# A second-level product for q's and k's first cells, decay products spaced further from their banks, and part of W_b's sums moved beside z

## The chip, the cores and the metric

The kernel runs on one core of one Trainium2 chip. Its time is the device time in microseconds of one execution; the times given are medians of several. All engines of the core run side by side: TensorE (PE in the profile, its weight loads PEld), VectorE (DVE), ScalarE (ACT), GpSimd (POOL), and SyncE (SP), which here does nothing but issue transfers.

## The reference

One layer of a decoder trunk for 1024 tokens and a model width of 1024. A combined projection of the normalised input gives all branches; branch A is a gated linear attention with decays, branch B a short gated convolution.

```python
h = rms_norm(x, norm_mix_g[i])
proj = jnp.einsum('bsd,dc->bsc', h, w_in[i])
(q, k, v, z_a, gk_low, cb, cc, xc, z_c, g_a, g_c) = jnp.split(proj, idx, axis=-1)
gk = log_sigmoid(gk_low @ w_gk2[i] + b_gk[i]) / GATE_NORMALIZER
o = gla_chunked(q, k, v, gk)                 # 4 heads, chunks of 64 tokens
y_a = (rms_norm(o, gla_norm_g[i]) * silu(z_a)) @ w_branch_a[i]
u = causal_dwconv(cc * xc, conv_w[i])
y_c = (cb * u * silu(z_c)) @ w_branch_c[i]
merged = sigmoid(g_a + b_ga) * y_a + sigmoid(g_c + b_gc) * y_c
x = x + merged @ w_out[i]
x = x + sigmoid(rms_norm(x, norm_ple_g[i]) @ w_ple_gate[i]) * (p[i] @ w_ple_proj[i])
return rms_norm(x, norm_final_g)
```

## The kernel before, in words

**Products.** Every large projection is done in quadrants by the Strassen-Winograd scheme: seven products of quadrant sums stand for eight. One product of one `Cell` is 12 matmuls 512 columns wide: four steps of 128 in the contraction, each of three matmuls (high by high, low by high, high by low part of operands that are split into two fp32r parts). A cell keeps three banks of PSUM: X, V and Y. Product 0 goes to X, product 1 to V, product 2 to Y (a copy of X), and DVE and ACT take the quadrants out of the banks as they are finished (`cons`). The weight sums of a product ("operand", with the names `T`, `raw`, `hi`, `lo`) are made by DVE and ACT up to seven products ahead, in a ring of eight.

**Second level.** `Deep` does one product of a pair of cells by seven smaller products, each of six matmuls of 256 columns: 42 of 256 in place of 24 of 512. It runs in two stages, one of 24 matmuls and one of 18, and between the two DVE adds four times and ACT copies twice on the banks (`dw` is the scratch tile, so `cc00dw` is the one of the pair cc0, xc0 for product 0). It needs "turned" quarters of h, which `quarters` loads.

**Phases.** In order of time: the norm and the small products until about 74 us; v (until 159 us) and z_a (tiles `za`, until 236.4 us), both by `wide`, which does four cells at once and stores z's silu; then q0 and k0 one after the other, q1 and k1 as a pair, the convolution's cells cc, xc, zc, cb in pairs until 596 us; the merge gates with the attention between them; then the branches' output products, the output projection and the gate of the per-layer embedding.

**The decays.** `decays(half)` makes `lowp`, 16 matmuls with the low-rank gate weights, and then four `zp`, one matmul each, whose banks DVE empties at once (`c<-zp`). They have a tag "o" with two banks, one of which the wide product beside them holds. `zp` and `lowp` are put between the matmuls of v and z.

**W_b.** The gate's weights (`wb`) are read in 16 pieces of 512 KB into the tile `wt`; each piece gets four subtractions of 128x256 and its sums are stored to `wtd` in DRAM, four stores of 128 KB (w = 0) or more (w = 1). In the kernel before, all 16 are woven in beside the convolution's cells.

**The order.** Nothing is issued as it is written: all operations are recorded (so that nearly all carry the line L508), `set_dues` gives each a due time counted back from the end, less its `hurry`, and `put_in_order` runs a small plan with costs per operation and puts each engine's instructions in the order of that plan. The order of the main matmuls is that in which they are recorded; the side ones (`lowp`, `zp`, attention) go in when the plan thinks they are ready, `apart` microseconds behind the release of their bank. `weave(generator, n)` records a generator's steps between products, so that `yield 7` waits seven of those steps. SP issues transfers in one queue.

Of the kernel before, what the change touches and what calls it, by code (L numbers as in the profile page):

```python
# [16 lines left out]
P = 128  # L17
# [502 lines left out]
def kernel(  # L520
# [216 lines left out]
    class Cell:  # L737
# [3 lines left out]
        def __init__(self, name, side, src, res, cons, prods=ORDER, begin=None, s1=None, u2=None, s5=None, fresh=(), mixed=False):  # L741
            self.name, self.side, self.src, self.res, self.cons = name, side, src, res, cons
            self.prods, self.begin, self.after = list(prods), begin, None
            self.get = {"u2": u2, "s5": s5}
            self.s1, self.seed, self.ready, self.halves = s1, None, lambda k: True, None
            self.raw, self.ring, self.order, self.Y, self.deep = [None] * 4, {}, None, None, {}
# [35 lines left out]
        def by_halves(self, k):  # L782
# [4 lines left out]
            for n, acc in enumerate((self.Y, self.Z)):  # L787
# [8 lines left out]
                else:  # L796
                    self.halves(0, n, acc[:, cs])

        def run(self, k):
            if k == self.prods[0]:  # L800
                if self.begin:
                    self.begin()
            if k == 0:
                self.X = bank(self, 0)
                self.product(0, self.X, True)
                self.Y = bank(self, 1)
                nc.scalar.copy(self.Y, self.X)
            elif k == 1:
                if self.seed is not None:
                    self.Y = bank(self, 1)  # L810
                    nc.scalar.copy(self.Y, self.seed)
                self.V = bank(self, 2)
                self.product(1, self.V, True)
                self.c22 = self.taken("s5", self.V)
            elif k == 2:
                self.product(2, self.Y, False)
                self.c12 = self.taken("u2", self.Y)
                if self.halves:
                    self.Z = psm.tile([P, 512], F32, tag=f"m{3 * (1 - self.set)}", name=f"{self.name}Z")
                    nc.scalar.copy(self.Z[:, 256:], self.Y[:, 256:])  # L820
            elif k == 3:
                self.product(3, self.X, False)
                self.cons(0, 0, self.X)
            elif k == 5:
                self.product(5, self.V, False)
                tt(self.c12, self.V, self.c12, op=ALU.add)
                self.cons(0, 1, self.c12)
# [12 lines left out]
    class Deep:  # L840
# [53 lines left out]
        def run(self, k):  # L894
# [16 lines left out]
            else:  # L911
# [3 lines left out]
                for c, t in ((a, self.a), (b, self.b)):  # L915
                    if self.k:
                        c.V = t
                        c.c22 = c.taken("s5", t)
                    else:
                        c.X = t  # L920
                    if self.k or 1 not in c.deep:
                        c.Y = bank(c, 1)
                        nc.scalar.copy(c.Y, c.X)

    def line_up(groups):
# [3 lines left out]
        todo = []  # L929
        for g in groups:  # L930
            own = [(g[s], k) for s, k in (g[0].order or [(s, k) for k in g[0].prods for s in range(len(g))])]
            if g[0].deep and 1 not in g[0].deep:
                todo.insert(len(todo) - 1, (g[0].deep[0], 0))
                own.insert(1, (g[0].deep[0], 1))
            elif g[0].deep:
                at = len(todo)
                g[0].deep[1].behind = [(c, j) for c, j in todo[-2:] if j == 6]
                for m, (k, n, left) in enumerate(((0, 0, 5), (0, 1, 3), (1, 0, 2), (1, 1, 0))):
                    todo.insert(at - left + m, (g[0].deep[k], n))
            todo += own  # L940
# [31 lines left out]
    def ev(name):  # L972
        return ep.tile([P, 512], F32, tag="ev", name=name, bufs=3)
# [222 lines left out]
    def wide(name, w, cons, first, second, more_s, more_u):  # L1196
# [89 lines left out]
        for b in range(4):  # L1286
            cons(1, 0, b, Y[b])

    with phase("v", [ph["prep0"]]) as qp:
        def v_cons(i, j, b, src):  # L1290
            hi = qp.tile([P, 512], F32R, tag="vhi", name=f"vhi{i}_{j}_{b}", bufs=2)
# [4 lines left out]

        def z_cons(i, j, b, src):
            t = ev(f"sz{i}_{j}_{b}")
            act(t, src, AF.Silu)
            store(szd[j][i][:, b], t.rearrange("p (h d) -> p h d", h=2))  # L1300

        smask = qp.tile([P, HALF], F32, name="smask")
# [5 lines left out]
        tt(gdif, graw[:, 4:8, :], graw[:, 0:4, :], op=ALU.subtract)  # L1308


        glw = qp.tile([P, 12, 4, 32], F32R, name="glw")
        for i in range(4):
            split(glw[:, 0:8, i, 0:16], glw[:, 0:8, i, 16:32], graw)
            split(glw[:, 8:12, i, 0:16], glw[:, 8:12, i, 16:32], gdif)
# [5 lines left out]
        def decays(half):  # L1320

            ops = ((0, 0), (4, 3)) if half == 0 else ((0, 1), (8, 6))
            lowp = pso.tile([P, 512], F32, tag="o", name=f"lowp{half}", bufs=2)
            n = 0
            for g0, k in ops:
                for kt in range(4):
                    gl = glw[:, g0 + kt, :, :].rearrange("p a b -> p (a b)")
                    for s in range(2):
                        mm(lowp, gl, hres[k][s][:, kt, :], start=n == 0, stop=n == 15)
                        n += 1  # L1330
            low = qp.tile([P, 512], F32R, tag="low", name=f"low{half}")
# [4 lines left out]
            for hp in range(2):  # L1336
                t1 = [qp.tile([P, HALF], F32, tag="t1", name=f"t1_{half}{hp}{i}", bufs=3) for i in range(2)]
                c = [qp.tile([P, HALF], F32, tag="c4", name=f"c4_{half}{hp}{i}", bufs=4) for i in range(2)]
                for i in range(2):
                    h = 2 * hp + i  # L1340
                    zp = pso.tile([P, 512], F32, tag="o", name=f"zp{half}_{h}", bufs=2)
                    cs = slice(h * P, (h + 1) * P)
                    nc.apart = 0.6
                    mm(zp, g2[:, cs], low, start=True, stop=True)
                    nc.apart, nc.hurry = 0.0, 6.0
                    nc.vector.tensor_scalar(c[i], zp, bgk[:, h:h + 1], None, op0=ALU.add)
# [53 lines left out]
        def extra():  # L1400
# [6 lines left out]
             [(ep, "ev", 3)] * 2, [(ep, "ev", 3), (qp, "wu", 1)])  # L1407
        finish_woven()
        weave(decays(1), 1)
        wide("za", [wv[1, n] for n in range(4)], z_cons, ("m3", "m4", "o", "m5"), ("m0", "m1", "o", "m2"),  # L1410
             [(qp, "vhi", 2)] * 2, [(qp, "vlo", 2)] * 2)
        finish_woven()
        qks = []
# [111 lines left out]
        convs = pairs(convs)  # L1525

    with vp:
        def weights(vp):


            def soon(do, *a, **kw):
                nc.hurry = 60.0
                do(*a, **kw)
                nc.hurry = 0.0

            for w in range(2):
                for kt in range(4):
                    for cs in (slice(0, 256), slice(256, 512)):
                        t = vp.tile([P, 4, 256], F32, tag="wt", name=f"wt{w}_{kt}_{cs.start}")
                        soon(load, t, wb[w][:, :, kt, cs].rearrange("n p c -> p n c"))  # L1540
                        yield 7
                        b11, b12, b22, b21 = (t[:, n] for n in range(4))
                        if w:
                            for n, q in enumerate((b11, b12, b22, b21)):
                                k = kt + 4 * (n >= 2)
                                soon(act, q, q, AF.Copy, scale=gple[:, k:k + 1])
                                if n != 1:
                                    soon(store, wtd[w][4 + (n + 1) // 2][:, kt, cs], q)
                        soon(tt, b11, b12, b11, op=ALU.subtract)
                        yield 1  # L1550
                        soon(tt, b12, b22, b12, op=ALU.subtract)
                        yield 1
                        soon(tt, b22, b22, b11, op=ALU.subtract)
                        yield 1
                        soon(tt, b21, b21, b22, op=ALU.subtract)
                        for n, q in enumerate((b11, b22, b12, b21)):
                            soon(store, wtd[w][n][:, kt, cs], q)
                        yield 2

        gas, gcs = ([Cell(f"{m}{c}", "B", W[f"{m}{c}"], hres, gate_cons(c, bias, dst), prods=(1, 2, 4, 5, 6),  # L1560
                          s1=s1d[n + c]) for c in range(4)]
                    for n, m, bias, dst in ((0, "ga", bga, gad), (4, "gc", bgc, gcd)))
        def quarters(k):
# [10 lines left out]
                back.append((th[:, n], tl[:, n]) if n < 3 or k else (at(hi, 0, 1), at(lo, 0, 1)))  # L1574
            yield 1
            for n in range(4):
                while n == 3 and not k and qks[1].Y is None:
                    yield 1
# [482 lines left out]
```

## Time and profile before

| | |
|---|---|
| median of 3 runs | 1074.16 us (1073.63 to 1074.26) |
| the profiled execution | 1074.43 us |
| its span | 1072.6 us |
| granted clock of TensorE | 0.998 of full speed |
| PE busy | 1063.1 us (99%) |
| DVE busy | 921.5 us (86%) |
| ACT busy | 650.1 us (61%) |
| POOL busy | 45.8 us (4%) |
| moved by DMA | 256.81 MB, 239 GB/s on average |

The profile has a timeline of each instruction (start, duration, engine, line, operation, output and inputs by tile name without buffer numbers, shape, and in brackets the idle time before it and who ended it), the chain of work that ended last, and windows with the busy time of each engine in a stretch (PE, PEld, DVE, ACT, POOL, then the clock, the share of the DMA engines that was busy and GB/s). An "x12" stands for twelve like rows. Matmuls overlap: a 512-wide one is drawn 0.39 us long although the next starts 0.227 us behind it, so distances from start to start count.

### The profile page before, as it was taken

To read this page: it belongs to the slowest core of one execution; us is meant where nothing else is said; L and a number is where in the kernel's file an instruction comes from. 1 tells how busy PE (TensorE), PEld (TensorE's weight loads), DVE (VectorE), ACT (ScalarE), POOL (GpSimd) and SP (SyncE) were. 2 spreads that over 40 slices of the span, in tenths; PEclk is the share of its full clock that TensorE was granted. 3 is DMA by queue.
4 is the path that set the end of the run, shared out by engine and by line. 5 is a ranking of instruction groups with operands and counts; after the bars stand their busy time and mean duration, and the time that the engine had idled before them with its cause. 6 is when DMAs were issued, how large, how long until landed. Compare 5 with 4: busy or idle time off the path is not lost.

```text
span 1072.6 us, 15816 instructions
## 1 busy us (share of the span) xinstructions
PE 1063.1 (99%) x5169; PEld 899.2 (84%) x5169; DVE 921.5 (86%) x1557; ACT 650.1 (61%) x1216; POOL 45.8 (4%) x83
## 2 busy tenths in 40 slices
PE   9999999999999999999999999999999999999996
PEld 7888888888888888888888888888888888888886
DVE  6998987658999998979889788886999888889896
ACT  6778648746654544565556477675766635466555
POOL 0000000000000000000000011120000000012021
PEclk9999999999999999999999999999999999999999
DMA  9963774468767545654557969889586779799963
GB/s 320 357 234 111 237 276 168 155 214 253 224 201 237 188 150 163 209 176 153 196 182 253 291 213 365 296 295 353 190 307 216 286 221 315 243 326 334 308 226 134
DMA packets 164866, 256.81 MB, mean 239 GB/s; under 512 B 13872, under 2 KB 79152, under 8 KB 161840
## 3 DMA queue, kind: packets, MB, share of 16 engines
q1 hardware_dynamic: 164640, 255.55, 70.6%
q8 instruction: 40, 0.66, 0.2%
q14 instruction: 42, 0.34, 0.1%
q10 hardware_dynamic: 144, 0.26, 0.1%
HBM read 166.63 MB, written 89.13 MB: 238 GB/s over the span
## 4 chain that ended last, share of the span: by engine, by line
PE 99%; DVE 0%; ACT 0%; issue 0%; POOL 0%; ACTq 0%; DVEq 0%
PE zaY L508 3%; PE vY L508 3%; PE pe L508 2%; PE vX L508 2%; PE zaX L508 2%; PE zaV L508 2%; PE vV L508 2%; PE op L508 2%; PE kv L508 1%; PE ga1Y L508 1%; PE ga0Y L508 1%; PE ga2Y L508 1%; PE cc2Y L508 1%; PE cc1Y L508 1%; PE cc3Y L508 1%; PE zc2Y L508 1%
## 5 line engine op out<-in xcount | busy, mean ns | idle before, releaser
L508 ACT ACT_TABLE_LOAD x21 | 26.9, 1283 | 1.1 <-PEq L2050 0.7
L508 DVE TENSOR_TENSOR wt<-wt 128x256 f32<-128x256 f32 x64 | 26.9, 421 | 0.2
L508 DVE SCALAR_TENSOR_TENSOR u<-t,vec,u 128x512 f32<-128x512 f32 x32 | 23.9, 750 | 1.8 <-ACT u L508 1.7
L508 ACT ACTIVATE junk<-x 128x512 bf16<-128x512 f32 (+1 forms) x30 | 18.0, 600 | 12.2 <-DVE x L508 11.8
L508 POOL MEMSET t<- 128x2 f32 x8 | 0.8, 99 | 443.9 <-DVE qdl L508 248.2
L508 POOL TENSOR_SCALAR rg<-ms 128x1 f32<-128x1 f32 x8 | 6.4, 796 | 258.8 <-ACT junk L508 258.7
L508 ACT ACTIVATE u<-t,vec 128x512 f32<-128x512 f32 x16 | 11.6, 727 | 6.8 <-DVE t L508 3.9
L508 ACT ACTIVATE og<-op,or 128x256 f32<-128x256 f32 x32 | 13.3, 469 | 2.2 <-POOL or L508 2.2
L508 ACT ACTIVATE junk<-op 128x256 bf16<-128x256 f32 x32 | 12.1, 380 | 3.0 <-PE op L508 2.9
L508 ACT ACTIVATE wt<-wt,vec 128x256 f32<-128x256 f32 x32 | 13.6, 498 | 0.0
L508 ACT CAST S<-S 128x512 fp32r<-128x512 f32 x14 | 8.7, 618 | 7.8 <-PE op L508 6.5
L508 ACT ACTIVATE oq<-oq,vec 128x512 f32<-128x512 f32 x20 | 13.2, 714 | 0.0
L508 PE MATMUL pe<-wpehi,pThi 128*128 128x512 f32 x32 | 13.0, 407 | 0.0
L508 POOL TENSOR_TENSOR or<-or,mhalf 128x2 f32<-128x2 f32 x16 | 12.8, 800 | 1.3
L508 DVE TENSOR_TENSOR szl<-og,szl 128x512 f32<-128x512 f32 x16 | 11.0, 688 | 2.2 <-ACT og L508 2.2
L508 PE MATMUL pe<-wpehi,pTlo 128*128 128x512 f32 x32 | 12.8, 401 | 0.0
L508 PE MATMUL pe<-wpelo,pThi 128*128 128x512 f32 x32 | 12.8, 401 | 0.0
L508 PE MATMUL op<-v,aTh 128*128 128x256 f32 x64 | 12.8, 283 | 0.0
L508 DVE SCALAR_TENSOR_TENSOR S<-S,dds,kv 128x256 f32<-128x256 f32 x24 | 10.4, 477 | 2.7 <-PE kv L508 2.3
L508 DVE TENSOR_TENSOR s<-y,s 128x512 f32<-128x512 f32 x16 | 11.0, 688 | 0.9 <-ACT s L508 0.7
L508 DVE SCALAR_TENSOR_TENSOR hq<-hq,vec,rt 128x512 f32<-128x512 f32 x16 | 11.2, 746 | 0.6 <-PE rt L508 0.6
L508 DVE STREAM_TRANSPOSE oT<-szl 128x512 f32<-128x512 f32 x16 | 11.3, 707 | 0.1
(3568 smaller groups left out, 4322.6 us busy)
## 6 DMA issues: line engine op xcount, KB each, us to landing
wtd<-wt SPq DMA_DIRECT2D x88, 128.0 KB, 2.8
wt<-in_wb_dram SPq DMA_DIRECT2D x16, 512.0 KB, 3.8
v<-vd SPq DMA_DIRECT2D x16, 512.0 KB, 6.0
wgq<-wtd SPq DMA_DIRECT2D x7, 1024.0 KB, 6.7
qk<-qkd SPq DMA_DIRECT2D x12, 512.0 KB, 6.4
vraw<-in_wv_dram SPq DMA_DIRECT2D x20, 256.0 KB, 3.7
zaraw<-in_wv_dram SPq DMA_DIRECT2D x20, 256.0 KB, 4.2
uq<-ud SPq DMA_DIRECT2D x5, 1024.0 KB, 6.2
```

What stands on the lines that cost most here:

```text
L508: o.call(*[place(a) for a in o.args], **{k: place(a) for k, a in o.kw.items()})
```

## The change

It has four parts.

1. q0 and k0 become a pair like q1 and k1, with a second-level product for product 0. The order of products is 1, 5, 2, 3, 4, 6, so both cells' V products run before the bank X is needed; the first stage stands behind the third product, the second behind the next two. Since product 5 comes early, the (0,1) quadrant is put together later, by the new `join`, from X, Y and V. The turned quarters no longer wait for k0's product 0. On PE, 24 matmuls of 512 columns become 42 of 256.
2. The decay's low-rank weights are kept once, and ACT copies them fourfold for each half (`glx`, in the buffer tag "wt"). The plan keeps `lowp`'s first matmul and each `zp` 1.0 us from the release of their bank, where it kept 0 and 0.6.
3. The first five pieces of W_b go beside z, through one buffer, the other eleven stay beside the convolution's cells; their `hurry` falls from 60 to 20.
4. z's first four banks get their tags in another order, and the silu of its first quadrant a `hurry` of 40.

```diff
+        def join(self):
+            self.c12 = self.taken("u2", self.X)
+            tt(self.c12, self.Y, self.c12, op=ALU.add)
+            nc.scalar.copy(self.Y, self.c12)
+            tt(self.c12, self.V, self.c12, op=ALU.add)
+            self.cons(0, 1, self.c12)
...
+            elif k == 2 and self.prods[1] == 5:
+                self.Y = bank(self, 1)
+                self.product(2, self.Y, True)
+                if self.X is not None:
+                    self.join()
...
-                    elif self.k or 1 not in c.deep:
+                    if c.prods[1] == 5:
+                        if c.Y is not None:
+                            c.join()
+                    elif self.k or 1 not in c.deep:
...
-            if g[0].deep and 1 not in g[0].deep:
+            if g[0].deep and g[0].prods[1] == 5:
+                own.insert(3, (g[0].deep[0], 0))
+                own.insert(6, (g[0].deep[0], 1))
+            elif g[0].deep and 1 not in g[0].deep:
...
+    pieces = [(w, kt, slice(c, c + 256)) for w in range(2) for kt in range(4) for c in (0, 256)]
...
+            nc.hurry = 20.0
...
+            nc.hurry = 0.0 if i or j else 40.0
             act(t, src, AF.Silu)
+            nc.hurry = 0.0
...
-        glw = qp.tile([P, 12, 4, 32], F32R, name="glw")
+        glw = qp.tile([P, 12, 32], F32R, name="glw")
...
+            glx = qp.tile([P, 8, 4, 32], F32R, tag="wt", name=f"glx{half}")
+            for n, (g0, _) in enumerate(ops):
+                nc.scalar.copy(glx[:, 4 * n:4 * n + 4], f(glw[:, g0:g0 + 4, None, :].to_broadcast([P, 4, 4, 32])))
...
+                        nc.apart = 0.0 if n else 1.0
                         mm(lowp, gl, hres[k][s][:, kt, :], start=n == 0, stop=n == 15)
...
-                    nc.apart = 0.6
+                    nc.apart = 1.0
                     mm(zp, g2[:, cs], low, start=True, stop=True)
...
+        weave(weights(qp, pieces[:5], 3), 2)
-        wide("za", [wv[1, n] for n in range(4)], z_cons, ("m3", "m4", "o", "m5"), ("m0", "m1", "o", "m2"),
+        wide("za", [wv[1, n] for n in range(4)], z_cons, ("m5", "m4", "o", "m3"), ("m0", "m1", "o", "m2"),
...
-                while n == 3 and not k and qks[1].Y is None:
-                    yield 1
...
-            for g in convs[1:] if k else pairs(qks[2:]) + convs:
+            for g in convs[1:] if k else pairs(qks) + convs:
                 Deep(g, k, turned[k], tq)
+        for c in qks[:2]:
+            c.prods = [1, 5, 2, 3, 4, 6]
...
-            weave(weights(vp), 10)
+            weave(weights(vp, pieces[5:], 7), 10)
...
-        run_groups(single(qks[:2]) + [qks[2:]] + convs, pairs(gas[:2]))
+        run_groups([qks[:2], qks[2:]] + convs, pairs(gas[:2]))
```

On VectorE, this stood between the two second-level stages of the convolution's first pair (`cc00dw` and `xc0X` belong to that stage, `Q` and `kk` to the consumers of q1 and k1; the number behind a name tells buffers of one name apart):

```order
L508 TENSOR_TENSOR cc0lo<-cc0T_3201,cc0hi 128x512
L508 TENSOR_TENSOR Q_1_3180<-q1s_2952,Q_1_3180 128x4x64
L508 TENSOR_TENSOR Q_1_3180<-q1s_2952,Q_1_3180 128x8x64
L508 TENSOR_TENSOR cc00dw<-cc0X,cc00dw 128x256
L508 TENSOR_TENSOR Q_1_3180<-Q_1_3180,dcs 128x4x64
L508 TENSOR_TENSOR xc0X<-xc0X,cc00dw 128x256
L508 TENSOR_TENSOR kk_1_3209<-k1s_3024,kk_1_3209 128x4x64
L508 TENSOR_TENSOR cc00dw<-cc0X,cc00dw 128x256
L508 TENSOR_TENSOR xc0lo<-xc0T_3275,xc0hi 128x512
L508 TENSOR_TENSOR xc0X<-xc0X,cc00dw 128x256
```

And this stands there now:

```order
L508 TENSOR_TENSOR cc0T_3373<-cc0raw_3095,cc0T_3273 128x512
L508 TENSOR_TENSOR xc0lo<-xc0T_3330,xc0hi 128x512
L508 TENSOR_TENSOR Q_1_3376<-q1Y,Q_1_3376 128x8x64
L508 TENSOR_TENSOR cc00dw<-cc0X,cc00dw 128x256
L508 STREAM_TRANSPOSE turned_0_3397<-kk_0_3185 128x4x4x32
L508 TENSOR_TENSOR xc0X<-xc0X,cc00dw 128x256
L508 TENSOR_TENSOR kk_1_3404<-ck_1_3313 128x4x2x64
L508 TENSOR_TENSOR cc00dw<-cc0X,cc00dw 128x256
L508 TENSOR_TENSOR Q_1_3376<-q1Y,Q_1_3376 128x4x64
L508 TENSOR_TENSOR xc0X<-xc0X,cc00dw 128x256
```

The four instructions of the stage (two `cc00dw`, two `xc0X`) are the same; what stands among them is a transpose of k1 and other parts of q1 and k1, and from the first `kk<-k0X` of k0 to the last row there are now 108 instructions, where there were 96.

On TensorE, this stood at the first `lowp` of the second half, in v's product 4:

```order
L508 MATMUL vV_1197<-v5hi_1316,h5lo 128x512
L508 MATMUL vY_1185<-v4hi_1320,h4hi 128x512
L508 MATMUL vY_1185<-v4lo_1332,h4hi 128x512
L508 MATMUL vY_1185<-v4hi_1320,h4lo 128x512
L508 MATMUL vY_1200<-v4hi_1320,h4hi 128x512
L508 MATMUL lowp_1530<-h1hi,glw 128x512
```

And now:

```order
L508 MATMUL vY_1193<-v4hi_1323,h4hi 128x512
L508 MATMUL vY_1193<-v4lo_1330,h4hi 128x512
L508 MATMUL vY_1193<-v4hi_1323,h4lo 128x512
L508 MATMUL vY_1199<-v4hi_1323,h4hi 128x512
L508 MATMUL vY_1199<-v4lo_1330,h4hi 128x512
L508 MATMUL vY_1199<-v4hi_1323,h4lo 128x512
L508 MATMUL vY_1255<-v4hi_1323,h4hi 128x512
L508 MATMUL lowp_1531<-h1hi,glx_1034 128x512
```

`lowp` stands behind seven matmuls of product 4, where it stood behind four.

On SyncE, this stood in z's first part (`zaraw` are the raw z weights, `vd` is where v is stored; buffers by number):

```order
L508 DMA zaraw_3_1769<-in_wv_dram 128x512
L508 DMA vd_1_1786<-vhi_0_0_1778 128x2x256
L508 DMA zaraw_0_1793<-in_wv_dram 128x512
L508 DMA vd_1_1786<-vhi_0_1_1788 128x2x256
L508 DMA vd_1_1786<-vlo_0_0_1797 128x2x256
L508 DMA zaraw_1_1814<-in_wv_dram 128x512
```

And now:

```order
L508 DMA zaraw_3_1776<-in_wv_dram 128x512
L508 DMA wt_0_256_1792<-in_wb_dram 128x4x256
L508 DMA vd_1_1801<-vhi_0_0_1786 128x2x256
L508 DMA vd_1_1801<-vhi_0_1_1798 128x2x256
L508 DMA zaraw_0_1818<-in_wv_dram 128x512
L508 DMA vd_1_1801<-vlo_0_0_1815 128x2x256
L508 DMA zaraw_1_1832<-in_wv_dram 128x512
```

The load of W_b's second piece stands ahead of the next raw z weights; the first piece's four stores stand further up.

More of the change, by code (lines that the diff above doesn't have):

```diff
@@ L745, in __init__ @@
             self.s1, self.seed, self.ready, self.halves = s1, None, lambda k: True, None
-            self.raw, self.ring, self.order, self.Y, self.deep = [None] * 4, {}, None, None, {}
+            self.raw, self.ring, self.order, self.deep = [None] * 4, {}, None, {}
+            self.X = self.Y = self.c12 = None
             (self.steps, self.operand), self.fresh = ring_steps(name, side, self.raw, fresh, mixed), fresh
@@ L825, in run @@
                 self.product(5, self.V, False)
-                tt(self.c12, self.V, self.c12, op=ALU.add)
-                self.cons(0, 1, self.c12)
+                if self.c12 is not None:
+                    tt(self.c12, self.V, self.c12, op=ALU.add)
+                    self.cons(0, 1, self.c12)
             elif k in (4, 6) and self.halves:
@@ L920, in run @@
                         c.X = t
-                    if self.k or 1 not in c.deep:
+                    if c.prods[1] == 5:
+                        if c.Y is not None:
+                            c.join()
+                    elif self.k or 1 not in c.deep:
                         c.Y = bank(c, 1)
@@ L1287, in wide, with weights, soon @@
             cons(1, 0, b, Y[b])
+    pieces = [(w, kt, slice(c, c + 256)) for w in range(2) for kt in range(4) for c in (0, 256)]
+    def weights(pool, some, pace):
+        def soon(do, *a, **kw):
+            nc.hurry = 20.0
+            do(*a, **kw)
+            nc.hurry = 0.0
+        for w, kt, cs in some:
+            t = pool.tile([P, 4, 256], F32, tag="wt", name=f"wt{w}_{kt}_{cs.start}")
+            soon(load, t, wb[w][:, :, kt, cs].rearrange("n p c -> p n c"))
+            yield pace
+            b11, b12, b22, b21 = (t[:, n] for n in range(4))
+            if w:
+                for n, q in enumerate((b11, b12, b22, b21)):
+                    k = kt + 4 * (n >= 2)
+                    soon(act, q, q, AF.Copy, scale=gple[:, k:k + 1])
+                    if n != 1:
+                        soon(store, wtd[w][4 + (n + 1) // 2][:, kt, cs], q)
+            soon(tt, b11, b12, b11, op=ALU.subtract)
+            yield 1
+            soon(tt, b12, b22, b12, op=ALU.subtract)
+            yield 1
+            soon(tt, b22, b22, b11, op=ALU.subtract)
+            yield 1
+            soon(tt, b21, b21, b22, op=ALU.subtract)
+            for n, q in enumerate((b11, b22, b12, b21)):
+                soon(store, wtd[w][n][:, kt, cs], q)
+            yield 2
     with phase("v", [ph["prep0"]]) as qp:
@@ L1298, in z_cons @@
             t = ev(f"sz{i}_{j}_{b}")
+            nc.hurry = 0.0 if i or j else 40.0
             act(t, src, AF.Silu)
+            nc.hurry = 0.0
             store(szd[j][i][:, b], t.rearrange("p (h d) -> p h d", h=2))
@@ L1308 @@
         tt(gdif, graw[:, 4:8, :], graw[:, 0:4, :], op=ALU.subtract)
-        glw = qp.tile([P, 12, 4, 32], F32R, name="glw")
-        for i in range(4):
-            split(glw[:, 0:8, i, 0:16], glw[:, 0:8, i, 16:32], graw)
-            split(glw[:, 8:12, i, 0:16], glw[:, 8:12, i, 16:32], gdif)
+        glw = qp.tile([P, 12, 32], F32R, name="glw")
+        split(glw[:, 0:8, 0:16], glw[:, 0:8, 16:32], graw)
+        split(glw[:, 8:12, 0:16], glw[:, 8:12, 16:32], gdif)
         g2raw = qp.tile([P, 512], F32, tag="low", name="g2raw")
@@ L1326, in decays @@
                 for kt in range(4):
-                    gl = glw[:, g0 + kt, :, :].rearrange("p a b -> p (a b)")
+                    gl = glx[:, n // 2].rearrange("p a b -> p (a b)")
                     for s in range(2):
+                        nc.apart = 0.0 if n else 1.0
                         mm(lowp, gl, hres[k][s][:, kt, :], start=n == 0, stop=n == 15)
@@ L1527 @@
     with vp:
[L1528 to L1549, printed above, removed]
-                        yield 1
[L1551 to L1558, printed above, removed]
         gas, gcs = ([Cell(f"{m}{c}", "B", W[f"{m}{c}"], hres, gate_cons(c, bias, dst), prods=(1, 2, 4, 5, 6),
@@ L1576, in quarters @@
             for n in range(4):
-                while n == 3 and not k and qks[1].Y is None:
-                    yield 1
                 for t, src in zip(back[n], tqd[k][n]):
```

## The prediction

> **What bounds the kernel now.** I read four views of the profile in this order: the busy times and the chain that ended last, TensorE's waits, the chain in order of time at the places that the change touches, and there the timelines of PE (TensorE) and DVE (VectorE).
>
> ```profile
> PE 1063.1 (99%) x5169; PEld 899.2 (84%) x5169; DVE 921.5 (86%) x1557; ACT 650.1 (61%) x1216; POOL 45.8 (4%) x83
> PE 99%; DVE 0%; ACT 0%; issue 0%; POOL 0%; ACTq 0%; DVEq 0%
> PE warm L508 <- DVE zero L508: 1.4, 1, 1.4
> ```
>
> PE is busy for 1063.1 of 1072.6 us and carries 99% of the chain; its one listed wait is 1.4 us at the very start. So the time can fall in two ways only: matmuls take less, or the small holes between them close. It rises by every microsecond that PE is made to wait. The profiled execution took 1074.43 us, its span 1072.6; 1.83 us lie outside the span and I leave them. It stands 0.27 above the median of 1074.16, so I add up against 1074.43 and take off 0.27 at the end.
>
> A full product's quadrant is 12 matmuls 512 columns wide. A second-level product replaces 24 of those by 42 matmuls of 256, in a stage of 24 and a stage of 18. Before has one for k1 and q1, shown here by the chain in order of time (start, duration, what):
>
> ```profile
> 236.38 2.72 PE q0X L508 x12
> 271.73 1.44 PE k1X L508 x12
> 273.17 1.44 PE q1X L508 x12
> 274.61 2.75 PE k0Y L508 x12
> 280.07 0.71 PE k1X L508 x6
> 280.79 1.44 PE q1X L508 x12
> 282.23 2.75 PE k1V L508 x12
> ```
>
> **The change: the pair.** 24 matmuls of 512 cost 2 x 2.72 = 5.44 us. The 42 of 256 cost 274.61 - 271.73 = 2.88 and 282.23 - 280.07 = 2.16; the 12 behind each stage take 2.75 instead of 2.72, 0.06 together. That is 5.10, a saving of **0.34 us** (0.43 if 42 matmuls went at the 18-matmul stage's 2.15 us without those 0.06). A rule speaks against it: the Trainium skill, page "TensorE: Matmul & The Clock Gate", section "Back-to-back issue gap", gives sustained spacings of about 81 ns for 128 columns and 131 for 512; half-width matmuls would then cost nearly as much as full ones, and, put on a line between the two, my estimate is 98 ns for 256 and a loss of 1.0 us. By the same section's isolated gap, N/2.4 + 2.5, it would be a gain of 0.59. The rows above lie between, at 227 ns and 120; they are of this very form, and decide.
>
> **The holes at the decay products.** PE's timeline (start, duration) and the DVE row that frees the bank:
>
> ```profile
> 132.89 1.28 DVE L508 TENSOR_TENSOR vu<-vV,vu 128x512 f32<-128x512 f32 x2
> 133.61 0.39 PE L508 MATMUL vY<-v4hi,h4lo 128*128 128x512 f32 x1
> 133.84 0.39 PE L508 MATMUL vY<-v4hi,h4hi 128*128 128x512 f32 x1
> 134.22 0.50 PE L508 MATMUL lowp<-h1hi,glw 128*128 128x512 f32 x1
> 134.56 0.40 PE L508 MATMUL lowp<-h1lo,glw 128*128 128x512 f32 x1
> 175.81 0.39 PE L508 MATMUL zaX<-za3hi,h3lo 128*128 128x512 f32 x1
> 176.04 0.47 PE L508 MATMUL zp<-low,g 128*128 128x512 f32 x1
> 176.35 0.39 PE L508 MATMUL zaX<-za3hi,h3hi 128*128 128x512 f32 x1
> L508 ACT CAST S<-S 128x512 fp32r<-128x512 f32 x14 | 8.7, 618 | 7.8 <-PE op L508 6.5
> ```
>
> Starts should stand 0.227 apart. `lowp1` starts 0.38 behind its predecessor, the matmul after it 0.34 behind: 0.27 us lost. DVE ends at 134.17, PE starts at 134.22, so that eviction held it, with a hand-off of 0.05. The new order puts `lowp1` three matmuls further back, 0.68 us, more than the 0.27 needed: **-0.27**. The last `zp` loses 0.31 - 0.227 = 0.08; two more matmuls now stand before it, so that hole goes too if the DVE chain before it has not slipped: **-0.08**. The extra broadcast copies of the decay weights are two of ACT per half, and ACT is 61% busy. Three fewer table loads free ACT alone. I cost both at nothing; if the copies' cover failed, `lowp` would wait at most for both, 2 x 0.62 us by the nearest ACT copy of 512 columns in the last row.
>
> **DVE behind the pair.** This is the first price. The new stage stands in a stretch where DVE has no spare time (window: length, PE, PEld, DVE, ACT):
>
> ```profile
> 266.30:317.63 51.33, 51.33 (x258) 43.80 (x258) 51.24 (x100) 28.14 (x58) 0.00 (x0) 1.00 0.69 215
> 266.33 1.02 DVE L508 TENSOR_TENSOR kk<-k0X,kk 128x256 f32<-128x256 f32 x2 [0.27 <-PE k0X L508]
> 267.27 0.41 DVE L508 TENSOR_TENSOR kk<-kk,dcs 128x256 f32<-128x256 f32 x1
> 267.60 0.69 DVE L508 TENSOR_TENSOR q1lo<-q1T,q1hi 128x512 fp32r<-128x512 f32 x1
> 268.20 1.09 DVE L508 STREAM_TRANSPOSE turned<-kk 128x512 f32<-128x512 f32 x1
> 315.87 0.44 DVE L508 TENSOR_TENSOR xc0X<-xc0X,cc00dw 128x256 f32<-128x256 f32 x1
> 317.63 0.28 PE L508 MATMUL xc0X<-h0hi,cc0xc00Bhi 128*128 128x256 f32 x1
> 318.66 0.17 DVE L508 TENSOR_TENSOR dds<-dcs 128x4 f32<-128x4 f32 x1
> 318.74 1.13 DVE L508 STREAM_TRANSPOSE turned<-kk 128x512 f32<-128x512 f32 x1
> ```
>
> At 266.33 DVE has just caught up with PE (it had waited 0.27 for `k0X`). From there it works without a pause until the second `xc0X<-xc0X,cc00dw` ends at 316.31, and PE's second stage for cc0 and xc0 needs that result at 317.63: a margin of 1.32 us. In the new order 108 DVE instructions stand from that `kk<-k0X` up to that `xc0X`, where 96 stood: five more of 512 columns, four more of 256, three more of 4. Start to start these take 0.60 (267.60 to 268.20), 0.33 (267.27 to 267.60) and 0.08 (318.66 to 318.74): 3.00 + 1.32 + 0.24 = 4.56. PE has one more product of 12 between the same two points, 2.72. The margin becomes 1.32 + 2.72 - 4.56 = -0.52, and with the hand-off of 0.05 PE waits **+0.57**. At full durations (0.69, 0.41, 0.17) the added work is 5.60 and the wait 1.6; if DVE comes to the first of these instructions earlier against PE than now (0.27 of waiting) and planned gaps fall well, it is near 0.2. I take 0.57. ACT has 23 us free in that window, which hides the added copy of the join. The turned quarters of h, which the new stage reads, no longer wait for k0's first product, so SP asks for them before any pair needs them.
>
> **Pieces of W_b beside z.** Each piece is a 512 KB load, four subtractions and four stores:
>
> ```profile
> L508 DVE TENSOR_TENSOR wt<-wt 128x256 f32<-128x256 f32 x64 | 26.9, 421 | 0.2
> wtd<-wt SPq DMA_DIRECT2D x88, 128.0 KB, 2.8
> 148.00:152.00 4.00, 4.00 (x19) 3.32 (x18) 4.00 (x8) 2.45 (x6) 0.00 (x0) 1.00 0.57 197
> 150.00:160.00 10.00, 10.00 (x45) 8.27 (x45) 6.41 (x11) 4.34 (x8) 0.00 (x0) 1.00 0.95 320
> 160.00:170.00 10.00, 10.00 (x45) 8.26 (x44) 8.24 (x14) 5.16 (x10) 0.00 (x0) 1.00 0.96 311
> 170.00:180.00 10.00, 10.00 (x45) 7.92 (x43) 10.00 (x18) 9.80 (x15) 0.00 (x0) 1.00 0.15 53
> 169.08 0.69 DVE L508 TENSOR_TENSOR zaT<-zaraw,zaT 128x512 f32<-128x512 f32 x1 [0.48 <-DMA zaraw<-in_wv_dram]
> 169.69 0.68 DVE L508 TENSOR_TENSOR vlo<-vY,vhi 128x512 fp32r<-128x512 f32 x1
> 170.29 0.74 DVE L508 TENSOR_SCALAR c<-zp,vec 128x512 f32<-128x512 f32 x1
> 171.20 0.40 PE L508 MATMUL zp<-low,g 128*128 128x512 f32 x1
> 155.75 0.65 SPq L508 DMA_DIRECT2D zaraw<-in_wv_dram  x1
> 163.79 0.36 SPq L508 DMA_DIRECT2D vd<-vlo  x1
> ```
>
> The 5 x 4 x 0.42 = 8.4 us of DVE leave a later place where PE does not wait, and gain nothing there. In z, DVE has room (82% busy), but the DMA engines do not: 0.95 and 0.96 busy until 170 us, then 0.15. The first piece's four stores and the second piece's load, 1.05 MB, now go into that full stretch ahead of the raw z weights that DVE already waits for at 169.08. At 311 to 320 GB/s they make these 3.3 us later, and about 2 if part of the stores fill the holes before 152 us (0.57 busy there). Weights as such have many microseconds of room; the second `zp` has not: its bank is freed by `c<-zp`, which DVE takes two instructions behind that `zaT`. Before, it ended at 171.03 and `zp` began at 171.20. After, `zaT` starts at 171.1 to 172.4 and `c` ends 1.95 later, 173.0 to 174.3. The new order has this `zp` ten matmuls later, less the 0.27 won: 171.20 + 2.27 - 0.27 = 173.20. PE waits between 0 and 1.1 us; I take the middle, **+0.5**. The two `zp` behind have 13 matmuls, 2.95 us, for five DVE instructions of some 0.6 (3.0 to 3.1), so they keep about the same lag. Below nothing this term can't go: nobody was held by W_b later.
>
> **Sum.** 1074.43 - 0.34 - 0.27 - 0.08 + 0.57 + 0.5 = 1074.81; less 0.27 is **1074.5 us**.
>
> **Rivals.** *All is hidden*: both waits fall away because DVE's order leaves it a microsecond more than my sums; then 1074.43 - 0.69 - 0.27 = **1073.5**. For it speaks that PE's rows show margins of this size met everywhere; against it, that DVE has no free time in the 51 us window.
>
> *SyncE's queue stands in z, and it is slower*: one buffer takes all pieces, so the second piece's load must wait until the first piece's stores have landed, and on SP's in-order queue the raw z weights stand behind it. If SP stood there for one store's 2.8 us on top of the 3.3, `zaT` would come 6.1 later, at 175.2, `c` would end at 177.1, and `zp` would wait 3.9 instead of 0.5: 1074.5 + 3.4 = **1077.9**. For it: that stretch is full and its transfers slow. Against: seven other DMAs are issued between the last store and that load, and SP takes 0.36 to 0.65 us for each, by the last two rows. It is over 0.2% slower once `zaT` comes more than about 4.4 us late.
>
> *The decay products keep their holes* because their banks come free as much later as they now stand: 1074.5 + 0.35 = **1074.9**.
>
> **How the numbers follow.** Chances: my forecast 0.55, all hidden 0.23, holes stay 0.07, SyncE stands 0.13; 0.02 for something unseen that gains more, as holes and pair together hold under 2 us. About 0.2%, 2.1 us, is what a measurement can tell from no change. So faster 0.02, same 0.85, slower 0.13. The low end, 1073.0, is the hidden case with 0.43 for the pair and most of the 0.5 by which the lowest run (1073.63) lies under the median; the high end, 1076.4, is the forecast with both waits at their upper bounds (1.6 and 1.1, so 1076.2) and the beginning of the slower rival.
>
> **What would show it.** Right: after `lowp1`, starts 0.227 apart; two more second-level stages of 2.88 and 2.16 us beside q0 and k0; a hole of about half a microsecond before the second stage of cc0 and xc0, with the `xc0X<-xc0X,cc00dw` of DVE ending 0.05 before it; a hole of up to 1.1 at the second `zp` of z, with the raw z weights landing 2 to 3 us later than now. Wrong: holes in other places (before q1Y or zc0's second stage), a hole of several microseconds in z, or none at all.

## The result: 1076.87 us, 0.26% slower

The changed kernel takes 1076.87 us (median of 10 runs, 1076.01 to 1077.61) beside 1074.05 of the kernel before on the same chip: a ratio of 1.0026, interval 1.0017 to 1.0036. The forecast was 1074.5 with a range up to 1076.4. The profiled execution took 1077.05 us, its span 1075.1.

The page of the changed kernel, busy times and chain:

```profile
PE 1063.4 (99%) x5187; PEld 899.3 (84%) x5187; DVE 926.0 (86%) x1563; ACT 649.7 (60%) x1215; POOL 45.7 (4%) x83
PE 67%; DVE 4%; issue 1%; ACT 0%; DMA 0%; POOL 0%; DVEq 0%; ACTq 0%
```

And TensorE's waits in it (in total, times, longest):

```profile
PE cb0X L508 <- DVE t L508: 1.7, 1, 1.7
PE X L508 <- DVE s L508: 0.4, 1, 0.4
PE xc0X L508 <- DVE xc0X L508: 0.2, 1, 0.2
```

Before, PE carried 99% of the chain and waited for nobody after the start. Now these three waits stand in the list besides that of the start, and the chain leaves PE. The largest is none that the prediction had priced: `cb0X`, the first second-level stage of zc0 and cb0, waits for a DVE product named `t`.

The timelines of DVE and PE there in the kernel before:

```profile
333.67 0.69 DVE L508 TENSOR_TENSOR t<-xc0X,t 128x512 f32<-128x512 f32 x1 [0.89 <-PE xc0X L508]
335.90 0.39 PE L508 MATMUL cc0V<-h5hi,cc0lo 128*128 128x512 f32 x1
336.13 0.28 PE L508 MATMUL cb0X<-turned0h,zc0cb00Shi 128*128 128x256 f32 x1
```

The timelines of PE, GpSimd, ACT and DVE in the changed kernel:

```profile
335.90 0.39 PE L508 MATMUL cc0V<-h5hi,cc0lo 128*128 128x512 f32 x1
337.99 0.36 PE L508 MATMUL cb0X<-turned0h,zc0cb00Shi 128*128 128x256 f32 x1 [1.70 <-DVE t L508]
338.18 0.28 PE L508 MATMUL cb0X<-turned0l,zc0cb00Shi 128*128 128x256 f32 x1
324.45 0.10 POOL L508 MEMSET t<- 128x2 f32 x1 [253.27 <-DMA qkd<-Q]
333.31 0.62 ACT L508 CAST cc0hi<-cc0T 128x512 fp32r<-128x512 f32 x1 [1.40 <-DVE cc0T L508]
334.43 0.58 ACT L508 COPY t<-cc0X 128x512 f32<-128x512 f32 x1
337.15 0.69 DVE L508 TENSOR_TENSOR t<-xc0X,t 128x512 f32<-128x512 f32 x1
```

`cb0X` takes over the bank that held xc0's X. DVE must first multiply that X into `t`, and ACT must before that copy cc0's X there. In the changed kernel DVE does so at 337.15 and ends at 337.84; PE starts 0.15 later, 1.86 late, and loses 0.08 more on the next matmul: 1.94 us. In the kernel before the same product ran at 333.67, as soon as PE had finished xc0's X (DVE stood idle 0.89 us for it), and ended 1.77 us ahead of PE.

The other holes (a hole is the time between two matmul starts beyond the usual 0.227 us, or 0.12 for 256 columns): 0.44 us at the second stage of cc0 and xc0, 0.18 at cc0's Y behind it, 0.23 at v's product 6 (from 147.30 us), and at the attention's first X (from 597.65 us) 0.67 more than the kernel before takes over the same matmuls. The two decay holes of before are closed. Two windows of the kernel before (columns as in the prediction) and the same of the changed one show where DVE's time went:

```profile
236.00:256.00 20.00, 20.00 (x90) 16.57 (x89) 12.79 (x27) 11.37 (x23) 0.00 (x0) 1.00 0.75 240
266.00:337.00 71.00, 71.00 (x358) 60.60 (x357) 68.80 (x133) 38.91 (x79) 0.20 (x2) 1.00 0.69 218
```

```profile
236.00:256.00 20.00, 20.00 (x110) 17.38 (x109) 11.50 (x23) 13.68 (x27) 0.00 (x0) 1.00 0.67 220
266.00:337.00 71.00, 70.11 (x347) 58.81 (x345) 71.00 (x142) 41.15 (x85) 0.20 (x2) 1.00 0.73 227
```

In the first 20 us of q0 and k0 DVE does less than before, 11.50 in place of 12.79; from 266 to 337 us it is busy to the last tenth, 71.00 of 71, where it had 2.2 us to spare. Single, q0 hands DVE its first quadrant at 249.67 us, before k0's first matmul at 255.25, and k0 follows at 266.33; as a pair, both cells' first quadrants come close together, from 260.28 and 262.96 us.

### The profile page after: what moved, and what is told of

It reads as the page before. It is cut to its first block, busy times and chain, and to the rows that moved or that the text cites. A ratio compares the mean times of both kernels' runs of the same rounds, so it can differ in the third digit from the quotient of the medians.

```text
span 1075.1 us, 15853 instructions
## 1 busy us (share of the span) xinstructions
PE 1063.4 (99%) x5187; PEld 899.3 (84%) x5187; DVE 926.0 (86%) x1563; ACT 649.7 (60%) x1215; POOL 45.7 (4%) x83
## 4 chain that ended last, share of the span: by engine, by line
PE 67%; DVE 4%; issue 1%; ACT 0%; DMA 0%; POOL 0%; DVEq 0%; ACTq 0%
PE op L508 2%; PE kv L508 1%; PE ga1Y L508 1%; PE ga0Y L508 1%; PE ga2Y L508 1%; PE cc3Y L508 1%; PE cc2Y L508 1%; PE zc0Y L508 1%; PE zc2Y L508 1%; PE zc1Y L508 1%; PE cc1Y L508 1%; PE gc0Y L508 1%; PE ga3Y L508 1%; PE zc3Y L508 1%; PE xc3Y L508 1%; PE cb2Y L508 1%
```

## The experiments

Each ratio is to the kernel before on the same chip, whose medians were 1073.60 to 1073.95 us. The theories. **A**: the pair puts q0's consumers behind k0's and DVE falls behind until 338 us. **B**: the pieces of W_b, moved and less hurried, upset the order. **C**: the plan thinks k's transposes shorter than they are (0.60 us for 1.02), so that its order is late in fact. **F**: `t` is placed behind q's and k's last work because it lies in memory that they used. **G**, against C and F: DVE has too much to do there in any order. The expectations name two more where they test them: **D**, that `t` stands behind the splits of later operands, or behind ACT, and **E**, that z's banks and the early silu let the pair start.

**The pair undone.** q0 and k0 are single again, all else as changed.

```diff
-        run_groups([qks[:2], qks[2:]] + convs, pairs(gas[:2]))
+        run_groups(single(qks[:2]) + [qks[2:]] + convs, pairs(gas[:2]))
...
-        for c in qks[:2]:
-            c.prods = [1, 5, 2, 3, 4, 6]
```

> The changed kernel with q0 and k0 single again; decays, W_b pieces and z's banks as changed. Theory A (the pair puts q0's consumers behind k0's, DVE falls behind from 260 to 338 us, and PE waits at xc0X, cc0Y and above all at the first second-level stage of zc0 and cb0): the holes there, 2.56 us in the changed kernel, are gone, none above 0.1 between 300 and 345 us; the two decay holes stay closed (-0.35), the new hole of 0.23 at v's product 6 and the 0.4 more at the attention's first X stay; about 1074.3. Theory B (the pieces of W_b in z and their lower hurry upset the order): the holes stay, about 1076.5 or more.

1074.34 us (ratio 1.0006, 0.9997 to 1.0014). No hole above 0.1 from 300 to 345 us, as A says; the hole at v's product 6 stays (0.22), the one at the attention's X is gone too, against the expectation. B falls as a cause of the holes from 300 to 345 us: the pieces are in z here as they are in the changed kernel, and PE waits for nobody after the start:

```profile
PE warm L508 <- DVE zero L508: 1.4, 1, 1.4
```

**The pair alone**, in the kernel before.

> The kernel before with the pair alone. Theory A: a hole of 1.5 to 2.5 us at the first second-level stage of zc0 and cb0, and one of some tenths at xc0X; 1074.05 - 0.34 + 1.5 to 2.6 = 1075.2 to 1076.3. Theory B: no such hole, 1073.7.

1084.21 us (1.0097, 1.0083 to 1.0111), worse than either theory had it. TensorE's waits:

```profile
PE zaY L508 <- ACT zaY L508: 3.5, 1, 3.5
PE k0V L508 <- ACT sz L508: 2.0, 1, 2.0
PE cb0X L508 <- DVE t L508: 0.7, 1, 0.7
PE cc0Y L508 <- ACT cc0Y L508: 0.3, 1, 0.3
```

The holes of A are there, smaller (0.95 and 0.57). But two greater ones stand before them: z's product 2 (the matmuls read `za2`; a later expectation calls it product 4) waits for ACT, and k0's V for ACT's silu `sz`, which still holds the bank that the second cell of the pair wants at once. z's new bank order and the silu's hurry, which I had passed over as costing nothing, looked like the remedy for that, so a later run adds them.

**No pieces in z.** All 16 are beside the convolutions, hurry 20.

```diff
-        weave(weights(qp, pieces[:5], 3), 2)
-            weave(weights(vp, pieces[5:], 7), 10)
+            weave(weights(vp, pieces, 7), 10)
```

> The changed kernel with all 16 pieces of W_b beside the convolutions (hurry 20 as changed). Theory A: the hole at the first stage of zc0 and cb0 stays within half a microsecond of 1.94 us; 1076.0 to 1076.9. Theory B: the holes go, about 1074. The hole at the attention's first X (0.67) tells whether it comes of the pieces: if so it is back at 0.25 or less.

1089.41 us (1.0147, 1.0131 to 1.0162). The hole at cb0X is the same 1.95 us, that at xc0X 0.45: theory A again. The hole at the attention's X is gone. The rest of the loss I had not foreseen; it stands far behind, at the products of the branch's output. The greatest wait there, and that at cb0X:

```profile
PE yc0X L508 <- ACT u0hi L508: 3.1, 1, 3.1
PE cb0X L508 <- DVE t L508: 1.7, 1, 1.7
```

PE comes there before the operand u0 is split. Five more waits of 0.6 to 1.4 us follow up to 791 us, for u0 to u3, and behind the first ones 13 matmuls run at about half the clock (last section): some 12 us together. With the low hurry alone the pieces don't fit beside the convolutions, while with a hurry of 60 they do (the pair with z's banks, below); so the five pieces in z and the hurry of 20 seem to belong together. The exact chain behind u0 was not followed.

**The price of a transpose.** The plan is told what the trace shows.

```diff
+            if op == "transpose" and o.name.startswith("turned"):
+                o.cost = 1.02
```

> The changed kernel; the plan prices the eight transposes of k at 1.02 us each, as measured, where it had 0.60. Theory C (DVE falls behind because the plan thinks its instructions shorter than they are, 0.42 us for each of k's transposes): DVE reaches the second stage of cc0 and xc0 four instructions earlier, the holes at xc0X and cc0Y (0.62) go, and that at zc0 and cb0 falls from 1.94 to about 1.3; 1075.5 to 1075.9. Without C (DVE simply has too much to do there): the holes together stay within 0.3 of 2.56, 1076.6 to 1077.

1078.06 us (1.0038, 1.0025 to 1.005). The holes at xc0X and cc0Y are gone, as C has it, but that at cb0X grew to 2.83, so that the sum is 0.27 above 2.56: the condition set for "without C". `t` still ran at 336.86, behind ACT's copy at 335.48. Alone, the price only moves the wait. The median lies above both ranges; the last section says what is known of that.

**Subtractions on GpSimd.** The first subtraction of every q and k consumer goes from DVE to GpSimd.

```diff
-                tt(kk[:, :, 0:4:3, :], c4, ...
+                nc.gpsimd.tensor_tensor(kk[:, :, 0:4:3, :], c4, ...
-                tt(d, c4[:, :, 0, :], ...
+                nc.gpsimd.tensor_tensor(d, c4[:, :, 0, :], ...
```

> The changed kernel; the first subtraction of each q and k quadrant's consumer (16 in all, of the loaded decays alone, 256 or 512 columns) is done by GpSimd in place of DVE. 15 DVE instructions fewer stand between k0's first consumer and the t that frees the bank, some 7 us. Theory A (DVE's load in that stretch makes the holes): the holes at xc0X, cc0Y and cb0X (2.56 us) go, about 1074.3. Rival D (the holes come of the order, t standing behind the splits of later operands, or of ACT): a hole of 1.5 us or more stays, 1076 or more.

1080.22 us (1.0056, 1.0042 to 1.007): a miss. The holes at xc0X and cb0X are gone, but q1's Y waits 4.1 us for DVE's `q1s`. The timelines of GpSimd, ACT and DVE show why DVE was not relieved:

```profile
287.44 3.60 POOL L508 TENSOR_TENSOR kk<-ck 128x512 f32<-128x512 f32 x1 [8.22 <-DVE qdl L508]
291.07 0.63 ACT L508 ACTIVATE kk<-kk 128x512 f32<-128x512 f32 x1 [2.07 <-POOL kk L508]
292.25 0.69 DVE L508 TENSOR_TENSOR k1lo<-k1T,k1hi 128x512 fp32r<-128x512 f32 x1 [2.11 <-ACT k1hi L508]
295.90 1.13 POOL L508 TENSOR_TENSOR kk<-ck 128x512 f32<-128x512 f32 x1 [4.29 <-DVE turned L508]
296.04 1.53 DVE L508 TENSOR_TENSOR qdl<-Q,qdh 128x512 fp32r<-128x512 f32 x1
297.50 0.68 DVE L508 TENSOR_TENSOR cc0xc00Slo<-cc0xc00S,cc0xc00Shi 128x512 fp32r<-128x512 f32 x1
```

A DVE instruction of 0.68 us takes 1.53 when GpSimd starts just ahead of it: the 1.13 us on GpSimd hold DVE up, and are longer than the 0.60 that DVE had been spared. Four DVE instructions between k0's first consumer and `q1s` are stretched so, by 2.8 us together. It goes the other way too: one subtraction takes 3.60 us on GpSimd beside a busy DVE (1.04 where it runs freely), ACT waits for it, and DVE then stands idle 2.11 us for ACT's `k1hi`. The Trainium skill, page "SBUF — State Buffer", section "SBUF: two separate sides", says that the two engines share a pair of ports as an exclusive lock which the loser waits for; these rows agree.

**Half of them**, the 256-wide ones alone.

> As the run before, but only the eight 256-wide subtractions of q's consumers go to GpSimd: eight DVE instructions fewer up to t, 8 x 0.33 = 2.6 us, three fewer up to xc0X, 1.0. Theory A: the holes at xc0X and cc0Y go, that at cb0X falls to between 0 and 0.6; 1074.3 to 1074.9. Rival D: 1076 or more.

1075.41 us (1.0013, 1.0004 to 1.0022), 1.5 below the changed kernel. The holes at xc0X, cc0Y and cb0X are gone and one of 0.98 at q1's Y is new: less work for DVE, shorter holes, though at another place than I had said.

**The pair with z's banks and silu**, in the kernel before.

> The kernel before with the pair and with z's changed bank order and the earlier silu, but decays and W_b as before. If z's banks and the silu are what lets the paired q0 and k0 start (theory E), the holes of 3.7 and 2.1 us that the pair alone had at z's product 4 and at k0V are gone and only those at xc0X, cc0Y and cb0X stay, 1 to 2.5 us: 1074.7 to 1076.0. If not, they stay: over 1080.

1076.03 us (1.0022, 1.0013 to 1.0031). The two large holes of the pair alone are gone: z's banks and the early silu are what makes the pair possible. What stays is 0.44, 0.11 and 1.94, nearly the changed kernel's own holes (0.44, 0.18, 1.94), without its decays and without pieces in z. PE's row at the last of them:

```profile
337.41 0.36 PE L508 MATMUL cb0X<-turned0h,zc0cb00Shi 128*128 128x256 f32 x1 [1.71 <-DVE t L508]
```

So the pair with its banks makes the loss at xc0X and cb0X by itself.

**GpSimd and the old hurry.**

> The subtractions on GpSimd, and W_b's pieces with their old hurry of 60. Expected: no holes from 300 to 345 us, and the attention's first X waits 0.25 us or less where it waited 0.67; 1073.3 to 1073.9, at or a little below the kernel before. If the hurry has nothing to do with that X, 1074.3.

1080.01 us (1.0058, 1.0045 to 1.0071): GpSimd's cost again, with 2.5 us at q1's Y and 0.66 at xc0X, where none was expected. The wait at the attention's X is gone, but so it was with GpSimd and the hurry of 20; it says nothing certain on the hurry.

**The first t outside.** Every second `t` lies in the pool that has been open since q and k.

```diff
-                t = rows_of[i, j] = vp.tile([P, HALF + 2], F32, tag="t", name=f"t{g}_{i}_{j}", bufs=2)
+                n = (i + j) % 2
+                t = rows_of[i, j] = (vp if n else tq).tile([P, HALF + 2], F32, tag=f"t{n}", name=f"t{g}_{i}_{j}")
```

> The changed kernel; every second tile t of the convolution is taken from the memory pool that is open since q and k, so that the first t no longer waits for q's and k's consumers to leave the memory that it reuses. Theory F (the 1.94 us at cb0X are that wait: GpSimd's memset, ACT's copy and DVE's product of the first t stand behind the last work on q1 and k1): t comes three DVE instructions earlier, 1.7 us, the hole at cb0X falls to about 0.3 and those at xc0X and cc0Y (0.62) stay; about 1075.2. Rival G (DVE simply has too much to do, whatever the order): 1.5 us or more stay at cb0X, 1076.5 or more.

1074.81 us (1.0006, 0.9997 to 1.0015). The hole at cb0X falls from 1.94 to 0.66, those at xc0X and cc0Y stay (0.37 and 0.09):

```profile
335.98 0.39 PE L508 MATMUL cc0V<-h5hi,cc0lo 128*128 128x512 f32 x1
336.76 0.39 PE L508 MATMUL cb0X<-turned0h,zc0cb00Shi 128*128 128x256 f32 x1 [0.39 <-DVE t L508]
```

F holds for most of the hole, though 0.3 was expected to stay.

**The first t outside, and the price.**

> As the run before, and the plan prices k's transposes at 1.02 us. Theory F with C: t comes eight DVE instructions earlier than in the changed kernel, xc0X four; no hole above 0.1 between 300 and 345 us; 1076.87 - 2.56 = 1074.3, with the attention's X perhaps at its 0.67 still. Rival G: the holes move but their sum stays near 2.6 as it did with the price alone.

1073.48 us (0.9996, 0.9987 to 1.0005). No hole above 0.1 from 300 to 345 us; G falls. The timelines of ACT, DVE and PE (the line is L510, since two were added):

```profile
329.75 0.59 ACT L510 COPY t<-cc0X 128x512 f32<-128x512 f32 x1 [1.45 <-PE cc0X L510]
332.48 0.69 DVE L510 TENSOR_TENSOR t<-xc0X,t 128x512 f32<-128x512 f32 x1
334.70 0.39 PE L510 MATMUL cc0V<-h5hi,cc0lo 128*128 128x512 f32 x1
334.93 0.28 PE L510 MATMUL cb0X<-turned0h,zc0cb00Shi 128*128 128x256 f32 x1
```

ACT's copy now waits for PE's X itself, DVE has `t` done at 333.17, and PE starts 0.23 behind its last matmul. DVE does the same work as in the changed kernel, 1563 instructions in all. Eight that stand before `t` there stand behind it here: q1's last `qdl`, k1's last transpose, five splits and sums for operands of later products, which D had named, and a small one.

**The same with hurry 60.**

> As the run before, with W_b's pieces at their old hurry of 60. No hole from 300 to 345 us; if the hurry makes the attention's first X wait, that falls from 0.67 to 0.25 or less: 1073.7 to 1074.3. Against it: earlier pieces fill DVE or the DMA engines at v's product 6, where the hole may grow from 0.23 to 1.

1073.87 us (0.9999, 0.999 to 1.0008). The wait at the attention's X (0.4 in the waits of the run before) is gone, and the holes at v's product 6 have grown from 0.21 to 1.2: both halves of the expectation, and the second is the larger.

**The pair without pieces in z.** Pair, z's banks, decays, t outside, price; W_b as before the change.

> The pair, z's banks and the decays of the change, the first t outside and the transposes' price; all W_b pieces beside the convolutions with hurry 60, as before the change. Theories A, C and F together: no hole that the kernel before has not, the two decay holes closed: 1073.8 - 0.34 - 0.35 = 1073.1, faster than the kernel before by 0.5 to 0.8 us. If the pair costs something that no hole shows, 1074 or more.

**1072.82 us** (1072.41 to 1073.32), 0.9989 of the kernel before (0.998 to 0.9998): the best of all, about 1.1 us below it. In the list of its waits PE waits for nobody after the start:

```profile
PE warm L510 <- DVE zero L510: 1.4, 1, 1.4
```

A hole of 0.20 at v's product 6, too small for this list, is here as well, which the expectation had not. So pair and decays account for -0.36 - 0.35 + 0.20 = -0.51 us. The other 0.6 comes of no wait: from the first matmul of cb0X to the first of zc3V the same matmuls take 238.76 us in the kernel before, 238.81 in the changed kernel, 238.55 with the price alone, 238.26 with the first t outside, and 238.14 in the three runs with both, because their starts stand a little closer throughout (256-wide ones 118.8 ns apart on average in place of 119.6). Why is open, and the kernel before was not run with the first t outside, so that this part can't be put down to the pair. The pair costs nothing that its holes don't show, and is worth its 0.36 us once they are closed.

## Why the prediction was wrong, point by point

**The pair's own price held.** From the start of q0's V to that of k1's V the changed kernel takes 45.49 us (235.92 to 281.41), the kernel before 45.85 over the same products: 0.36 less, 0.34 predicted. The stages take 2.87 and 2.15. The sustained spacings of the Trainium skill, page "TensorE: Matmul & The Clock Gate", section "Back-to-back issue gap", by which the pair would lose an estimated 1.0 us, don't hold for these matmuls. The measured spacings, 227 and 120 ns, don't lie between the two sets of figures that the prediction quotes, as it says, but above both; what lies between the two outcomes is the saving.

**The decay holes closed as said** (0.35), with something in their place that I had not looked for: v's product 6 starts 0.15 late and its second matmul 0.08. That hole comes with the new decays: the pair with banks, whose decays are as before, has not got it, and the run without pieces in z has. Whether their spacing or their copies make it was not tried apart. The first matmuls of the second `lowp` now stand about 0.23 apart:

```profile
134.22 0.40 PE L508 MATMUL vY<-v4hi,h4hi 128*128 128x512 f32 x1
134.46 0.40 PE L508 MATMUL lowp<-h1hi,glx 128*128 128x512 f32 x1
134.70 0.40 PE L508 MATMUL lowp<-h1lo,glx 128*128 128x512 f32 x1
```

**DVE behind the pair: the mechanism was right, the ledger stopped too early.** It gave 0.57 us at the second stage of cc0 and xc0, and 0.44 came, with 0.18 right behind:

```profile
316.75 0.39 PE L508 MATMUL cc0V<-h1hi,cc0lo 128*128 128x512 f32 x1
317.31 0.39 PE L508 MATMUL xc0X<-h0hi,cc0xc00Bhi 128*128 128x256 f32 x1 [0.17 <-DVE xc0X L508]
```

But I closed the account at that stage, at 108 instructions against 96. The first stage of zc0 and cb0 behind it needs the bank that `t` frees, and up to `t` the order has 148 instructions against 127. The 1.77 us of margin there, which the trace of before shows at 336.13, were not in my list. This is the step that failed; it cost 1.94 us. The prediction's own prices would have shown it: the 21 instructions (eleven of 512 columns, seven of 256, three of 4) make 6.60 + 2.31 + 0.24 = 9.15 us, against 1.77 of margin, 2.72 of PE and 1.85 that DVE stood idle between the two points before. That leaves a wait of 2.81, where 2.56 came in all (0.44 + 0.18 + 1.94). Part of it could be seen in the order, part in the plan: it lets `t` begin only when q's and k's memory is given up, which in the trace it need not (GpSimd's memset of that `t` runs at 324.45, ten us before ACT's copy), and it counts 0.60 us for each of k's transposes of 1.02.

**Pieces beside z cost nothing there.** I took +0.5. The windows and rows of the changed kernel:

```profile
160.00:170.00 10.00, 10.00 (x46) 8.27 (x45) 8.51 (x16) 4.98 (x10) 0.00 (x0) 1.00 0.99 330
170.33 0.69 DVE L508 TENSOR_TENSOR zaT<-zaraw,zaT 128x512 f32<-128x512 f32 x1
171.53 0.74 DVE L508 TENSOR_SCALAR c<-zp,vec 128x512 f32<-128x512 f32 x1
173.22 0.39 PE L508 MATMUL zp<-low,g 128*128 128x512 f32 x1
```

The raw weights' `zaT` comes 1.25 us later than before, not 2 to 3.3: the DMA engines went to 0.99 busy and 330 GB/s. `c` ends at 172.27 and `zp` starts at 173.22, where I had put it (173.20), with 0.95 to spare. The slower rival, SyncE standing still, did not happen; that the time came near its 1077.9 is chance. What makes the attention's first X wait 0.67 stays open: the two runs that put the hurry back to 60 and keep DVE clear have no such wait, but neither has the run with the pair undone, where pieces and hurry are as changed, nor the one without pieces in z, where the hurry is 20 too.

**The sum as it came**: 1074.43 - 0.36 - 0.35 + 0.23 + 0.44 + 0.18 + 1.94 + 0.67 = 1077.18, beside 1077.05 of the profiled execution. The rival that I had set on the slower side lay in z; the loss came of the same backlog that the forecast had priced, one bank further on. A range that held it would have needed that bank's wait as a term of its own.

## What to carry to other kernels

When work moves on a saturated engine, carry the account on to every later point where the bottleneck waits for that engine, banks that must be emptied included, until the engine has idle time again; the first place that you check need not be the one that pays. If a planner sets the order, compare its prices with the trace and look at what it believes to be blocked: a tile in reused memory was planned late here although the memory was open. And undo each part alone: here one part (z's banks and silu) was the remedy for another, the pair, and the best time came without a third, the pieces beside z.

## What was not expected of the hardware

**A long wait costs more than itself.** In the pair alone, PE's timeline after the wait of 3.5 us:

```profile
193.17 0.39 PE L508 MATMUL zaY<-za2hi,h2lo 128*128 128x512 f32 x1
197.10 0.80 PE L508 MATMUL zaY<-za2hi,h2hi 128*128 128x512 f32 x1 [3.54 <-ACT zaY L508]
197.70 0.63 PE L508 MATMUL zaY<-za2lo,h2hi 128*128 128x512 f32 x1
198.13 0.63 PE L508 MATMUL zaY<-za2hi,h2lo 128*128 128x512 f32 x1
```

The window from 197.00 to 200.20 us of the same run (length, PE, PEld, DVE, ACT, POOL, clock, share of DMA, GB/s):

```profile
197.00:200.20 3.20, 3.10 (x8) 2.48 (x9) 1.21 (x2) 1.69 (x5) 0.00 (x0) 0.52 1.01 330
```

The matmuls that follow start 0.43 apart in place of 0.227, and it takes seven of them until the spacing is back, some 1.5 us on top. The granted clock was 0.52 in that window, and 1.00 from 200.20 to 204.00 us. Holes of 2.1 and 2.4 us in these runs have no such tail. The run with the transposes' price, whose profiled hole is 2.8 us, took 1075.94 us with a granted clock of 0.998 over the whole execution, and 1077.4 to 1078.9 in its other executions, in three of four at 0.994 to 0.996. That the clock gave way behind the same hole there is likely, but not shown: the profile is of its fastest execution.

**GpSimd and DVE hold each other up**: 1.53 us for a DVE instruction of 0.68, and 3.60 for a GpSimd one of 1.04, by the rows above.
